# A hybrid stream encoder on one core: the order of the first loads, and the tiles that hold layer 0's last sums

## The chip, the cores and the metric

One Trainium2 chip, one of its cores. The metric is the device time of one execution of the whole program, in microseconds (us), as the median of several runs. A profiled execution gives the span (first to last instruction) and every instruction in it. The engines are called as in the profile: PE is TensorE (PEld its weight loads), DVE is VectorE, ACT is ScalarE, POOL is GpSimd, SP is SyncE, which issues most of the loads and stores of this kernel. A name with a q behind it (SPq, POOLq) is the sequencer of an engine, where DMA issues and waits are recorded.

## What is computed

One step of an encoder with two layers over 1024 prompt frames and 8 x 16 sample frames of width 1024. Layer 0 has its own keys and values and attends over a short window; layer 1 reads keys and values projected once, and attends over eight chunks of 64 before its own. Each layer ends in an MLP with squared ReLU. Cut to what matters here:

```python
def rmsnorm(x, g):
    xf = x.astype(jnp.float32)
    y = xf * lax.rsqrt(jnp.mean(xf * xf, axis=-1, keepdims=True) + EPS)
    return (y * g.astype(jnp.float32)).astype(x.dtype)

def mlp(x, g_norm, w_up, w_down):
    return jnp.square(jax.nn.relu(rmsnorm(x, g_norm) @ w_up)) @ w_down

for layer in range(DEPTH):
    if layer < N_LAYERS_A:
        qp, kp, vp = project_a(hp, g_attn[layer], w_qkv_a[i], g_q_a[i], g_k_a[i])
        ...
    else:
        kb_p, vb_p = shared_kv(hp, g_kv, w_kv, g_k_b)
        ...
    hp = hp + ap @ w_o
    hp = hp + mlp(hp, g_mlp[layer], w_up[layer], w_down[layer])
```

Everything is float32. `hp` is the residual of the prompt; the sample frames take the same steps.

## The kernel before

**Tiles.** The 1024 prompt frames are tiles 0 to 7 of 128 rows, the 128 sample frames are the ninth, `ST`. A matrix that feeds PE is split into a rounded high half and the rest as low half, and a product is made of three matmuls (high by high, high by low, low by high); `split` (L128 and L134) makes the halves, one on ACT or POOL, the other on DVE.

**The norm vectors.** The norm weights g are not applied to x but to the rows of the weight matrices. For this `prep_gains` (L1234) loads the five vectors (`g_attn` and `g_mlp` of both layers, `g_kv`) with five loads (L1243) into a tile of 40 x 128, turns it with a PE transposition (L1245) and copies it into `gcol` (L1246), one column for each 128 rows of each vector. The tile and its PSUM bank come from pools of their own, which are closed when the function ends; what is allocated next may come to lie in their place. The transposition needs the identity matrix: `run` loads it into `eye` (L1278), and DVE casts it to `identr` (L1280). All transpositions of x use it too.

**A weight.** `load_block` (L141) loads a weight in blocks of 256 rows (two k of 128) by 512 columns into a `raw` tile (L146). The raw tiles come from two pools in turn, `rawp` and, in layer 0, `ring` (tag `raw2`), two buffers each. `split_g` (L180) then multiplies each k with its column of `gcol`: the high half on POOL (L185), the low half on DVE (L190).

**The start of attention.** In layer 0, `attention` first calls, in this order of the code: `X(0)` (L1421, the load of x tile 0), the first block of the key and value weight, `X(1)`, `N(0)`, the second block, `X(ST)`, `N(1)`, the blocks three and four, `N(ST)`. `N` turns a tile of x (L210, eight transpositions), splits it into `hh` and `hl`, takes its sum of squares on ACT (Square, L201) and makes the scales of the tokens (L202, L1250 and L1254, the last on POOL). Then the constants follow (`sinks`, L1344 to L1353). The key and value projections `K1` of tiles 0, 1 and `ST` are interleaved: for each k the three matmuls of tile 0, then those of tile 1, and so on (L217 to L219). The query projections `Q1` of the same three tiles follow, with a weight of their own, then more tiles, scores and the rest of attention.

**Who orders the work.** The instructions of each engine are put in order at compile time, by a scheduler that runs a simulated timeline (`schedule_with_timeline_sim=True`); the engine then works its queue off in that order. `behind(a, b)` (L747) puts b after a in that order without making it wait for anything on the chip. A tile that takes the place of another one waits until the last reader of that one has finished (`reuse_waits="tile"`).

**The end of the MLP.** `mlp_down` multiplies with `w_down` in 40 products over two halves of the inner dimension, where sums of tokens and weights are formed so that fewer multiplications are needed. Each product has three banks (token tiles of a part; the parts are `PARTS = ((5, 6, 7), (2, 3, 4), (ST, 0, 1))`) and adds its result, with a sign, to some of six outputs o: output o belongs to part o // 2 and to the column half o % 2. The outputs are summed in SBUF tiles `x0` to `x8` where these are opened, and else the result is copied by ACT (L1162) and added to the residual in DRAM by a POOL DMA that accumulates (L1165 and L1179). The last two results are those of product 37 (output 0) and, in layer 0, of product 39, the last one (output 1). Both go, in the three token tiles of part 0, into the x tiles of part 2, which are done by then:

```python
if n > max(last[1:]) + 1:
    adds[o] = [xs[t][:, N[o % 2]] for t in PARTS[2]]
```

so into `x8` (`ST`), `x0` and `x1`. In layer 1 output 1 is opened at product 33 and does not come this way. `DOWN_HOME` (a list of tags) fixes which tile lies behind which in SBUF: ... `x8`, `x0`, `x2`, a gap of 640, `a0`, `x1`, `x3`, `x4` ... When layer 0 is over, the pools of layer 1's attention take the same place, in the order raw, weights, small tiles, `hpool` (`hh`, `hl`), work, ring, `apool` (`pth`, `ptl`, ...). By the sizes, `hh` and `hl` come to lie where `x8` and `x0` were, and `pth` and `ptl`, in which tile 1 is held, where the end of `x1`, `x3` and `x4` were.

## Time and profile before

| | us |
|---|---|
| median of 3 runs | 2357.6 |
| lowest and highest of them | 2350.82, 2359.93 |
| the profiled execution: its own time | 2354.01 |
| the profiled execution: span | 2352.2 |

The granted TensorE clock, as the mean of the profiled execution, was 0.997. Over the whole span the page shows these groups as the longest, with busy time, mean duration and idle time of the engine just before them:

```profile
L744 PE MATMUL ps_c<-w,a 128*128 128x512 f32 x960 | 374.7, 390 | 6.9 <-DVE w L134 6.9
L908 POOL DMA_DIRECT2D hd<-h x272 | 148.9, 550 | 594.8 <-ACT h L817 378.2
L128 ACT CAST a<-a 128x1536 fp32r<-128x1536 f32 x80 | 118.6, 1482 | 149.5 <-DMA a<-hd 149.5
L134 DVE TENSOR_TENSOR a<-a 128x1536 fp32r<-128x1536 f32 x80 | 140.5, 1756 | 45.7 <-ACT a L128 45.7
```

How such a line is read: the line of the kernel, the engine and operation, the tile written and the tiles read, the shape, how often; then busy us and mean ns of one; then how long the engine stood idle just before these instructions, and what it was released by. A row of a timeline has the start in us, the duration, the engine and the line; several alike instructions that follow each other are one row with their count. A row of the chain of waits has start, duration and what the time was spent in; "DMA a<-b" is a transfer from its issue until it let the next instruction go. Matmul durations overlap, so the pace of PE is the distance of two starts.

### The profile page before, as it was taken

Reading aid. Unit: us, or ns where it says so; the run is one execution under the profiler, and the core shown is the slowest. Engines: PE = TensorE matmul, PEld = TensorE weight load, DVE = VectorE, ACT = ScalarE, POOL = GpSimd, SP = SyncE. Lnnn points to the kernel's source line nnn. Section 1 sums busy time; section 2 is a strip of 40 time slices with the busy share of each in tenths; the row PEclk is TensorE's granted clock in tenths of the full one; section 3 lists DMA queues with packets and bytes.
Section 4 is the critical chain, followed back from the end, with each engine's and each line's share of the span. In section 5 each row is a group of like instructions: output and inputs, shape, how many; then the busy total and the mean of one; then the engine's idle time right before and its main releaser. Section 6 shows DMA issues by size and latency. Waiting matters only on the chain.

```text
span 2352.2 us, 33396 instructions
## 1 busy us (share of the span) xinstructions
PE 2271.4 (97%) x11429; PEld 1893.3 (80%) x11429; DVE 1715.4 (73%) x3075; ACT 1332.4 (57%) x2684; POOL 635.3 (27%) x950
## 2 busy tenths in 40 slices
PE   7998999899999999999999999998899999999999
PEld 6787887788888888777877788887788888888787
DVE  6788786766656578899577877777666566678987
ACT  3777674655555555344377666665655555565443
POOL 4334332313213111002333434344132132110011
PEclk9999999999999999999999999999999999999999
DMA  7335546234434677748653655555244343977567
GB/s 253 127 113 163 171 147 202 95 122 160 137 111 151 218 230 177 267 147 214 183 157 113 193 157 177 174 168 184 69 156 138 113 162 107 284 209 199 175 169 192
DMA packets 226715, 392.70 MB, mean 167 GB/s; under 512 B 51592, under 2 KB 126288, under 8 KB 226448
## 3 DMA queue, kind: packets, MB, share of 16 engines
q1 hardware_dynamic: 188816, 283.58, 37.4%
q0 software_dynamic: 36432, 102.26, 15.9%
q10 hardware_dynamic: 1296, 4.72, 0.5%
q8 instruction: 90, 1.47, 0.2%
q14 instruction: 81, 0.66, 0.1%
HBM read 236.51 MB, written 156.85 MB: 167 GB/s over the span
## 4 chain that ended last, share of the span: by engine, by line
PE 74%; DVE 9%; DMA 9%; ACT 3%; issue 3%; POOL 1%; SPq 0%; ACTq 0%; DVEq 0%; POOLq 0%
PE ps_c L743 6%; PE ps_c L744 6%; PE ps_c L745 6%; PE ps_x L743 5%; PE ps_x L745 5%; PE ps_x L744 5%; PE ps_mm L217 3%; PE ps_mm L219 3%; PE ps_mm L218 3%; PE ps_y L745 2%; PE ps_y L743 2%; PE ps_y L744 2%; PE ps_tr L324 2%; DMA a<-hd 2%; DVE w L134 1%
## 5 line engine op out<-in xcount | busy, mean ns | idle before, releaser
L744 PE MATMUL ps_c<-w,a 128*128 128x512 f32 x960 | 374.7, 390 | 6.9 <-DVE w L134 6.9
L743 PE MATMUL ps_c<-w,a 128*128 128x512 f32 x960 | 375.1, 391 | 5.1 <-DVE x L1174 3.1
L745 PE MATMUL ps_c<-w,a 128*128 128x512 f32 x960 | 374.3, 390 | 0.0
L908 POOL DMA_DIRECT2D hd<-h x272 | 148.9, 550 | 594.8 <-ACT h L817 378.2
L743 PEld LDWEIGHTS ps_c<-w,a 128*128 128x128 f32 x960 | 180.6, 188 | 46.3 <-issue 4.7
L744 PEld LDWEIGHTS ps_c<-w,a 128*128 128x128 f32 x960 | 180.7, 188 | 46.1 <-DVE w L134 9.0
L745 PEld LDWEIGHTS ps_c<-w,a 128*128 128x128 f32 x960 | 180.5, 188 | 37.5
L128 ACT CAST a<-a 128x1536 fp32r<-128x1536 f32 x80 | 118.6, 1482 | 149.5 <-DMA a<-hd 149.5
L217 PE MATMUL ps_mm<-w,hh 128*128 128x512 f32 x432 | 172.7, 401 | 8.8 <-POOL w L185 3.3
L134 DVE TENSOR_TENSOR a<-a 128x1536 fp32r<-128x1536 f32 x80 | 140.5, 1756 | 45.7 <-ACT a L128 45.7
L219 PE MATMUL ps_mm<-w,hl 128*128 128x512 f32 x432 | 171.7, 398 | 1.5 <-DMA hl<-hTd 1.4
L218 PE MATMUL ps_mm<-w,hh 128*128 128x512 f32 x432 | 170.8, 396 | 1.3 <-DVE w L190 1.1
L743 PE MATMUL ps_x<-sx,w 128*128 128x512 f32 (+1 forms) x408 | 157.8, 387 | 3.7 <-ACT h L864 2.7
L128 ACT CAST w<-s 128x2048 fp32r<-128x2048 f32 x56 | 107.1, 1912 | 92.2 <-DVE s L1060 80.7
L128 ACT CAST w<-ru 128x512 fp32r<-128x512 f32 (+1 forms) x160 | 110.0, 708 | 83.9 <-PE ps_y L744 32.0
L745 PE MATMUL ps_x<-sx,w 128*128 128x512 f32 (+1 forms) x408 | 154.1, 378 | 0.0
L744 PE MATMUL ps_x<-sx,w 128*128 128x512 f32 (+1 forms) x408 | 154.1, 378 | 0.0
L134 DVE TENSOR_TENSOR w<-s,w 128x2048 fp32r<-128x2048 f32 x56 | 128.1, 2288 | 32.4 <-ACT w L128 32.3
L1179 POOL DMA_DIRECT2D xp<-o x28 | 36.3, 1296 | 411.8 <-ACT o L1162 390.2
L134 DVE TENSOR_TENSOR ptl<-ps_tr,pth 128x512 fp32r<-128x512 f32 x180 | 122.4, 685 | 24.1 <-ACT pth L128 18.2
L134 DVE TENSOR_TENSOR w<-ru,w 128x512 fp32r<-128x512 f32 (+1 forms) x160 | 126.6, 793 | 14.7 <-ACT w L128 14.6
L816 ACT ACTIVATE h<-h 128x512 f32<-128x512 f32 (+1 forms) x102 | 61.9, 607 | 122.6 <-DVE h L866 93.5
(274 smaller groups left out, 6131.4 us busy)
## 6 DMA issues: line engine op xcount, KB each, us to landing
a<-hd SPq DMA_DIRECT2D x80, 768.0 KB, 6.2
hd<-h POOLq DMA_DIRECT2D x272, 192.0 KB, 2.5
ru<-in_w_up SPq DMA_DIRECT2D x64, 512.0 KB, 3.9
r<-in_w_down SPq DMA_DIRECT2D x32, 1024.0 KB, 10.0
xp<-o POOLq DMA_DIRECT2D x28, 768.0 KB, 9.4
o<-oTd SPq DMA_DIRECT2D x50, 256.0 KB, 5.0
x<-xp SPq DMA_DIRECT2D x23, 512.0 KB, 5.2
xp<-xo SPq DMA_DIRECT2D x18, 512.0 KB, 2.8
```

The costliest lines, as they stand in the source:

```text
L128: a = nc.scalar.copy(hi, src)
L134: return a, e.tensor_tensor(lo, src, hi.bitcast(F32), ALU.subtract)
L217: nc.tensor.matmul(ps, a, w[:, 0, k, :], start=(k == 0), stop=False)
L218: nc.tensor.matmul(ps, a, w[:, 1, k, :], start=False, stop=False)
L219: self.lp = nc.tensor.matmul(ps, b, w[:, 0, k, :], start=False, stop=(k == KC - 1))
L324: self.lp = nc.tensor.transpose(pt[:, i, :], get(i), self.ident)
L743: a = mm(ps, ah, bh, start=first, stop=False, skip_group_check=True)
L744: mm(ps, ah, bl, start=False, stop=False, skip_group_check=True)
L745: return a, mm(ps, al, bh, start=False, stop=last, skip_group_check=True)
L816: a = nc.scalar.activation(t, src, AF.Relu)
L908: return lambda p, z: self.nc.gpsimd.dma_start(self.hd[c // 4][:, p, c % 4], z)
L1179: nc.gpsimd.dma_start(dst, z, accum_op=ALU.add)
```

## The change

Two places. In the opening, the identity is no longer loaded in `run`. `prep_gains` is called from `attention` right behind `X(0)`, loads the identity, then the five vectors with three loads (both layers of `g_attn` in one, both of `g_mlp` in one, `g_kv`), all put behind x tile 0 in SP's order. Its tile is now a slot of the scratch tag of `work`, its bank the `m` bank of attention. The first weight block is put behind the last of these loads, and x tile 1 behind the first weight block. In `mlp_down`, the results of the very last product go into the x tiles 1, 3 and 4 instead of `ST`, 0 and 1; what they are added to in DRAM stays the same.

```diff
@@ load_block
-            nc.sync.dma_start(raw, wr[:, k0 : k0 + 2, n0 : n0 + 512])
+            self.ld = nc.sync.dma_start(raw, wr[:, k0 : k0 + 2, n0 : n0 + 512])
@@ mlp_down
-                            adds[o] = [xs[t][:, N[o % 2]] for t in PARTS[2]]
+                            home = (1, 3, 4) if n == total - 1 else PARTS[2]
+                            adds[o] = [xs[t][:, N[o % 2]] for t in home]
@@ prep_gains
-    def prep_gains(self):
+    def prep_gains(self, first):
         nc, I = self.nc, self.ins
-        with ExitStack() as st:
-            self.psum_pools(st, "pg", dict(m=(1, 1)), dict(m="m"))
-            tmp = self.pool(st, "tmpg")
-            g = tmp.tile([5 * KC, P], F32, tag="g", name="g")
-            for i, v in enumerate(
-                (I["g_attn"][0], I["g_attn"][1], I["g_mlp"][0], I["g_mlp"][1], I["g_kv"])
-            ):
-                nc.sync.dma_start(g[i * KC : (i + 1) * KC, :], v.rearrange("(k p) -> k p", p=P))
-            ps = self.psum("m", [P, 5 * KC], "ps_g")
-            nc.tensor.transpose(ps, g, self.ident[0 : 5 * KC, 0 : 5 * KC])
-            nc.vector.tensor_copy(self.gcol, ps)
+        z = [nc.sync.dma_start(self.eye, I["eye"])]
+        nc.vector.tensor_copy(self.identr, self.eye)
+        g = self.scratch([P, 4, P], F32, "g")[0 : 5 * KC, 0]
+        rows = lambda a: a.rearrange("l (k p) -> (l k) p", p=P)
+        z.append(nc.sync.dma_start(g[0 : 2 * KC], rows(I["g_attn"])))
+        z.append(nc.sync.dma_start(g[2 * KC : 4 * KC], rows(I["g_mlp"])))
+        z.append(nc.sync.dma_start(g[4 * KC : 5 * KC], I["g_kv"].rearrange("(k p) -> k p", p=P)))
+        for a in z:
+            self.behind(first, a)
+        ps = self.psum("m", [P, 5 * KC], "ps_g")
+        nc.tensor.transpose(ps, g, self.ident[0 : 5 * KC, 0 : 5 * KC])
+        nc.vector.tensor_copy(self.gcol, ps)
+        return z[-1]
@@ run
-            eye = cp.tile([P, P], F32, tag="eye", name="eye")
-            nc.sync.dma_start(eye, I["eye"])
+            self.eye = cp.tile([P, P], F32, tag="eye", name="eye")
             self.identr = cp.tile([P, P], F32R, tag="identr", name="identr")
-            nc.vector.tensor_copy(self.identr, eye)
...
-            self.prep_gains()
@@ attention
-                nc.sync.dma_start(xr[t], x_src(t))
+                return nc.sync.dma_start(xr[t], x_src(t))
...
-                X(0)
+                z = self.prep_gains(X(0))
                 self.load_block(wkv, wkv_src, kv0, gkv, [0])
-                X(1)
+                self.behind(z, self.ld)
+                self.behind(self.ld, X(1))
                 N(0)
```

## The prediction

> **What bounds the kernel now.** I read the page's busy shares first, then the windows over the opening and over the border between the two layers, then the timeline of each engine and the chain of waits there.

> ```profile
> span 2352.2 us, 33396 instructions
> PE 2271.4 (97%) x11429; PEld 1893.3 (80%) x11429; DVE 1715.4 (73%) x3075; ACT 1332.4 (57%) x2684; POOL 635.3 (27%) x950
> ...
> 0.00:4.20 4.20, 0.00 (x0) 0.01 (x1) 0.29 (x2) 1.28 (x1) 0.41 (x5) 1.00 0.16 32
> 4.20:6.50 2.30, 0.30 (x1) 0.17 (x1) 0.20 (x1) 0.04 (x1) 0.00 (x0) 1.00 0.91 333
> 10.40:13.50 3.10, 0.00 (x0) 0.00 (x0) 2.42 (x4) 0.44 (x1) 3.02 (x5) 1.00 0.94 352
> 13.50:15.80 2.30, 1.22 (x2) 0.50 (x2) 2.30 (x4) 0.00 (x0) 2.30 (x3) 1.00 0.48 170
> 15.80:20.00 4.20, 4.17 (x11) 3.33 (x12) 4.20 (x8) 1.15 (x2) 2.72 (x3) 1.00 0.41 140
> 20.00:35.00 15.00, 15.00 (x72) 12.48 (x71) 8.86 (x19) 3.12 (x7) 5.37 (x9) 1.00 1.05 394
> 35.00:54.60 19.60, 17.85 (x88) 14.69 (x86) 12.79 (x28) 7.46 (x19) 11.05 (x11) 1.00 0.56 173
> ```

> The columns of a window are its length, then busy time of PE, PEld, DVE, ACT and POOL, granted clock, DMA share, GB/s. TensorE is busy 97% of the span, so time is to be had only where it idles: 2352.2 - 2271.4 = 80.8 us in all. The first 4.2 us move 32 GB/s, and from 10.4 to 13.5 TensorE does nothing at all while the DMA engines are 94% busy. From 20 to 35 it has no gap. A start that comes earlier is therefore worth what it brings forward, if the stage after it stays fed.

> ```profile
> 0.74 0.39 SPq L1278 DMA_DIRECT2D eye<-in_eye  x1
> 2.94 0.83 SPq L1421 DMA_DIRECT2D x<-in_x_prompt  x2
> 3.81 0.43 SPq L146 DMA_DIRECT2D raw<-in_w_qkv_a  x1
> ...
> 2.60 1.49 DMA g<-in_g_kv
> ...
> 4.22 0.31 PE ps_g L1245
> ...
> 4.55 7.19 DMA raw<-in_w_qkv_a
> ...
> 2.64 0.23 DVE L1280 CAST identr<-eye 128x128 fp32r<-128x128 f32 x1 [1.76 <-DMA eye<-in_eye]
> 6.57 3.65 PE L210 MATMUL ps_n<-identr,x 128*128 128x128 f32 x16 [2.06 <-DMA x<-in_x_prompt]
> 7.70 0.59 ACT L128 CAST hh<-ps_n 128x512 fp32r<-128x512 f32 x1
> 10.48 1.36 POOL L185 TENSOR_SCALAR w<-raw,gcol 128x512 fp32r<-128x512 f32 x2 [2.02 <-DMA raw<-in_w_qkv_a]
> 11.81 0.98 POOL L1254 TENSOR_TENSOR rx<-vx,mhalf 128x1 f32<-128x1 f32 x1
> 12.78 0.69 POOL L185 TENSOR_SCALAR w<-raw,gcol 128x512 fp32r<-128x512 f32 x1
> 13.50 5.56 DVE L190 SCALAR_TENSOR_TENSOR w<-raw,gcol,w 128x512 fp32r<-128x512 f32 x5
> 13.52 1.22 PE L217 MATMUL ps_mm<-w,hh 128*128 128x512 f32 x2 [3.30 <-POOL w L185]
> 15.83 0.79 PE L218 MATMUL ps_mm<-w,hh 128*128 128x512 f32 x1 [1.08 <-DVE w L190]
> ```

> Two things are seen. The identity and five norm rows are issued before x, so x is issued at 2.94. And the second weight load is issued at 4.55, just as the transposition of the norm rows ends: the chain runs from g over ps_g to that load. I read this as the norm tile of `prep_gains` lying where the first `raw` buffer comes to lie. So the load that could go at 3.81 is the block in the other buffer (`raw2`, rows k = 2, 3), and the first block, k = 0, 1, is the one of 4.55, which lands at 4.55 + 7.19 = 11.74. The matmuls agree: the first one starts not after the two weight products of 10.48 but after the third (12.78 + 0.69 = 13.47), and its low half waits for the third L190 (five of them take 5.56, so 13.50 + 2 x 1.1 = 15.7).

> **The change, part one: the opening.** Moved to the front: x tile 0, from 2.94 to 0.74. Behind it in SP's queue come the identity, three norm loads instead of five, the first weight, x tile 1. Six issues filled 0.74 to 2.94, 0.37 us each: identity 1.1, norms 1.5 to 2.2, first weight about 2.6, x tile 1 about 3.0. Nothing is queued behind a wait, since none of these waits for an engine.

> x tile 0 was used at most 6.57 - 2.94 = 3.6 us after its issue, so it lands at about 4.3. The identity took 2.64 - 0.74 = 1.9 us alone; now its bytes follow x's, so 4.5, cast 0.23, and the transpositions start at 4.75 instead of 6.57: 1.8 us earlier. The high half of tile 0, at 7.70 to 8.29 before, is then done by 6.5.

> The norm rows land by about 4.6 (1.49 us after the last issue, and behind x), plus 0.31 for ps_g and 0.2 for its copy: 5.1 instead of 4.75. That is later, and costs nothing as long as the first weight lands after it, a cover of about 1 us; without the cover it costs up to that 0.4. Two fewer loads on SP save 0.7 us of issue, which is in the times above. The scratch slot and the one bank of PSUM that the norm rows now borrow are free again by 5.1, before the first projection wants them.

> Four loads of 512 KB landed between 6.5 (x 0) and 11.74 (first weight), so (11.74 - 6.5) / 3 = 1.75 us each. Now: x 0 at 4.3, the first weight at 6.2, x 1 at 8.0, the other weights at 9.7, 11.5, 13.2. The first weight product ends at 6.2 + 0.69 = 6.9, its low half on DVE at 8.0. The projections of tiles 0 and 1 are interleaved row by row, so PE then stands at tile 1: x 1 at 8.0, the 1.2 us that passed between tile 0's landing (6.5) and its first cast (7.70), and the cast of 0.59 give 9.8, and the low half on DVE about 10.4. What is late next is therefore x tile 1, no longer the weight. The steady stream that began at 15.83 begins at about 10.4: 5.4 us earlier. DVE does not hold it: its product takes 1.1 us for a row that gives PE six matmuls.

> ```profile
> 24.86 9.33 DMA raw<-in_w_qkv_a
> ...
> 34.27 1.36 POOL w L185 x2
> ...
> 29.58 0.47 ACT L276 ACTIVATE VS<-ps_mm,rx 128x256 fp32r<-128x256 f32 x1 [0.66 <-PE ps_mm L219]
> 16.42 0.63 PE L219 MATMUL ps_mm<-w,hl 128*128 128x512 f32 x1
> 16.84 0.63 PE L218 MATMUL ps_mm<-w,hh 128*128 128x512 f32 x1
> 19.54 0.39 PE L219 MATMUL ps_mm<-w,hl 128*128 128x512 f32 x1
> 19.77 0.40 PE L217 MATMUL ps_mm<-w,hh 128*128 128x512 f32 x1
> ```

> Does the next stage stay fed? Tiles 0 and 1 are projected by 29.58; the sample tile's 24 matmuls at 19.77 - 19.54 = 0.23 us follow, to about 35; then the queries, whose last weight pair is wanted 18 matmuls later, about 39. It lands at 34.2, and a product of 0.69 and a low half of 1.1 later, about 36, it can be used. The slack is 3 us. So if the query weights come no earlier than now, 3.0 us of the 5.4 survive; the DMA engines are full there (394 GB/s from 20 to 35), but only 140 to 170 GB/s were moved between 13.5 and 20, and the raw buffers come free earlier with the products. I take 5.0, with 3.0 as the low bound and, from the first weight product (13.47 to 6.9), 6.6 as the high one.

> **Part two: the last sums of layer 0.** They occur once, at the last of 40 products; in layer 1 the half concerned is already opened there, so nothing changes.

> ```profile
> 1135.52 0.86 POOL L1165 DMA_DIRECT2D xp<-x  x1 [7.10 <-ACT x L1162]
> 1138.30 0.85 POOL L1165 DMA_DIRECT2D xp<-x  x1 [1.92 <-ACT x L1162]
> 1139.87 1.94 PE L210 MATMUL ps_n<-identr,x 128*128 128x128 f32 x16
> 1141.11 0.85 POOL L1165 DMA_DIRECT2D xp<-x  x1 [1.96 <-ACT x L1162]
> 1142.63 1.07 ACT L128 CAST hh<-ps_n 128x512 fp32r<-128x512 f32 x2 [1.96 <-DMA xp<-x]
> 1143.36 0.47 PE L217 MATMUL ps_mm<-w,hh 128*128 128x512 f32 x1 [1.55 <-ACT hh L128]
> 1147.84 1.08 ACT L128 CAST hh<-ps_n 128x512 fp32r<-128x512 f32 x2 [4.14 <-DMA xp<-x]
> ```

> Three adds into DRAM read the tiles of the sample and of 0 and 1; layer 1's first `hh`/`hl` take the place of the first two, so ACT waits 1.96 us for an add to land and PE 1.55 us for ACT. With the sums in tiles 1, 3 and 4 those two places are last read two products earlier (the sums of the other half), and ACT can cast at 1142.63 - 1.96 = 1140.67. Gain at most 1.55. What is late next: the second tile's casts wait for the third add, landed at 1147.84, and by the sizes in the code tiles 3 and 4 lie where these buffers come to lie, so that wait stays. PE, starting its 24 matmuls (5.5 us) at 1141.8, would be done at 1147.4 and then stand about 0.6 to 1.1 us. Number of copies and adds unchanged: 0. Bounds 0 and -1.55; I take -1.0.

> **Sum.** -5.0 - 1.0 = -6.0 us against the profiled execution's 2354.0 (span 2352.2), so 2348.0; the median of the runs shown, 2357.6, stands 3.6 above it, so 2351.6, given as 2351.5. From the bounds alone: 2357.6 - 8.15 = 2349.5 to 2357.6 - 3.0 = 2354.6.

> **Rivals.**

> Late query weights: the part-one gain stops at the slack of 3.0 and the border gives nothing: 2354.6. For it: DMA share 1.05 from 20 to 35. Against: the low traffic before 20.

> [...]

> ```profile
> 400.00:450.00 50.00, 43.71 (x260) 36.33 (x259) 43.02 (x63) 28.57 (x52) 21.11 (x18) 1.00 0.31 109
> ...
> 1600.00:1700.00 100.00, 88.04 (x537) 75.35 (x536) 68.00 (x102) 56.63 (x117) 32.40 (x31) 0.97 0.34 114
> ```

> Another order further on. The order of the queues is chosen by a simulated timeline, which starts differently now, and attention's order may come out otherwise. These two rows are the largest stalls, 6.3 and 12.0 us of PE idle. A new stall like the larger, added to -6.0, gives +6.0: 2363.6; it decides from 6 us up. The same effect with luck, one stall of 6.3 closed besides: -12.3, 2345.3. Nothing in the profile speaks for either; most later stages are chained to PE and would only move.

> The change does not do what it says: the norm tile still holds back a weight, x 0 alone gains 1.8, its use waits for the weight: 2357.

> **How the numbers follow.** Forecast 0.50; late query weights 0.14; colder start 0.04; another order, slower 0.11, faster 0.16; not done 0.05. The likeliest gives 2351.5, its own range 2349.5 to 2354.6 before the spread of medians (the runs shown span 9 us, so about 4 each way). With the other cases the range is 2340 to 2362. 0.5% is 11.8 us, about what a measurement of this kernel can tell from no change. Faster than 2345.8: most of the lucky order and the tail of the forecast, 0.23. Slower than 2369.4: a stall beyond 18 us, 0.06. Within: 0.71.

> **What would show it.** x 0 issued at about 0.74 and transposed at about 4.8; the first weight product at 6 to 7, the first matmul near 7, the stream from about 10.4, and the projections of tiles 0 and 1 done near 24 instead of 29.6. At the border ACT's first cast not released by the add, the idle of 1.55 gone and a smaller one before the second tile. The forecast is wrong if the stream begins after 13, if PE idles between 24 and 40, or if the border's and the opening's gains are seen but the stages between them have other lengths.

## The result and the profile after

The change made the kernel slower. Ten runs of the changed kernel have a median of 2368.07 us (2360.59 to 2377.28), ten of the kernel before 2357.74 (2350.82 to 2362.4): ratio 1.0047, 95% interval 1.003 to 1.0064. Nine more runs of it, beside 33 of the kernel before, gave 1.0035 (1.002 to 1.005). The mean of the two ratios is 1.0041, some 9.7 us of loss where 6 of gain were forecast.

The busy shares of the page of the changed kernel; its profiled execution took 2371.51 us, at a mean granted clock of 0.988:

```profile
span 2369.7 us, 33389 instructions
PE 2287.0 (97%) x11429; PEld 1907.0 (80%) x11429; DVE 1716.9 (72%) x3075; ACT 1330.7 (56%) x2684; POOL 633.6 (27%) x950
```

TensorE's idle time is 2369.7 - 2287.0 = 82.7 us, only 1.9 more than before, while the span is 17.5 longer. The rest is busy time: the same 11429 matmuls kept TensorE busy for 15.6 us more. Hold on to that; it is the half of the answer that an idle count doesn't show.

The opening, in the timeline of the changed kernel (start, duration, engine, line, work, and in brackets the idle time before it with its releaser):

```profile
0.74 0.38 SPq L1421 DMA_DIRECT2D x<-in_x_prompt  x1
2.58 0.37 SPq L1243 DMA_DIRECT2D g<-in_g_kv  x1
2.99 0.41 SPq L146 DMA_DIRECT2D raw<-in_w_qkv_a  x1
...
5.97 0.30 PE L1247 MATMUL ps_g<-identr,g 40*128 40x40 f32 x1 [5.97 <-DMA g<-in_g_kv]
6.20 1.97 PE L210 MATMUL ps_n<-identr,x 128*128 128x128 f32 x8
8.04 0.78 PE L217 MATMUL ps_mm<-w,hh 128*128 128x512 f32 x1
10.17 0.77 PE L218 MATMUL ps_mm<-w,hh 128*128 128x512 f32 x1
...
25.13 0.50 PE L219 MATMUL ps_mm<-w,hl 128*128 128x512 f32 x1 [2.27 <-DVE hl L134]
...
50.58 0.66 PE L260 MATMUL ps_q<-identr,qr 128*128 128x128 f32 x4 [1.80 <-DVE qr L239]
```

The stream of matmuls starts at 10.17 instead of 15.83, and the first transpositions of queries, at 54.65 in the timeline of before, stand at 50.58: 4.1 us earlier. The opening does what it was meant to do.

Where the lead goes is read by following some instructions, found by their line and their number on it, through both timelines:

| start of | before | after | difference | after, second execution | difference |
|---|---|---|---|---|---|
| first transposition of queries (L260) | 54.65 | 50.58 | -4.1 | 50.67 | -4.0 |
| first probability product (L331) | 71.13 | 68.63 | -2.5 | 67.10 | -4.0 |
| last probability product of layer 0 (L332) | 374.55 | 384.01 | +9.5 | 380.15 | +5.6 |
| first product of the MLP (L743, `ps_x`) | 430.78 | 435.42 | +4.6 | 431.56 | +0.8 |
| last sum product of layer 0 (L745, `ps_c`) | 1139.64 | 1149.51 | +9.9 | 1145.87 | +6.2 |
| first probability product of layer 1 | 1198.48 | 1216.18 | +17.7 | 1209.61 | +11.1 |
| end of the span | 2352.2 | 2369.7 | +17.5 | 2363.2 | +11.0 |

The second execution is the profile of whole_change_again, the same kernel. Two stretches lose that the change has reordered: the attention of layer 0 (up to the first product of the MLP) and the border of the layers. The attention's loss must not be read at its last probability product: the new order only puts that product later, 51.4 us ahead of the MLP where before has 56.2. The MLP between the two stretches is longer too, by 5.2 and 5.5 us, though its order is the same; over the 14 profiles of this study it takes 708.9 us (before, the shortest of all) to 716.1, so how much of that is chance stays open. Behind the border nothing more is lost.

Windows (length, then busy time of PE, PEld, DVE, ACT, POOL, granted clock, DMA share, GB/s), first two of before, which go with the rows of before in the prediction:

```profile
300.00:400.00 100.00, 95.79 (x509) 78.12 (x508) 73.14 (x206) 61.94 (x167) 31.16 (x53) 1.00 0.57 187
1140.00:1199.00 59.00, 55.18 (x286) 46.11 (x285) 37.66 (x103) 27.32 (x75) 22.83 (x33) 1.00 0.65 207
```

Then the changed kernel:

```profile
300.00:400.00 100.00, 90.91 (x463) 73.17 (x462) 65.34 (x183) 54.96 (x152) 28.28 (x50) 0.97 0.52 167
400.00:450.00 50.00, 46.23 (x260) 37.59 (x258) 44.48 (x65) 28.63 (x52) 21.27 (x20) 1.00 0.35 127
1600.00:1700.00 100.00, 87.96 (x527) 74.94 (x526) 71.96 (x124) 58.15 (x129) 37.45 (x37) 0.95 0.38 127
1140.00:1217.00 77.00, 70.19 (x331) 59.10 (x330) 40.15 (x105) 29.27 (x77) 25.80 (x35) 0.91 0.53 159
```

At 300 to 400 and at the border TensorE both idles more and runs at a lower clock: 0.97 and 0.91 as the mean of these windows, against 1.00 in before. In the 14 profiles of this study, from 30 us on, the lower clock comes as stretches of one or two times 3.41 us at 0.50 to 0.52, and outside of them it is 0.98 to 1.00 (the last section); half pace means these stretches. The two places in the timeline, first the attention, one row of before and three of the changed kernel:

```profile
364.47 0.47 PE L176 MATMUL ps_mm<-w,oh 128*128 128x512 f32 x1 [1.55 <-DVE xo L1614]
```

```profile
351.12 0.50 PE L176 MATMUL ps_mm<-w,oh 128*128 128x512 f32 x1 [2.04 <-DVE xo L1614]
367.55 0.47 PE L176 MATMUL ps_mm<-w,oh 128*128 128x512 f32 x1 [1.76 <-DVE xo L1614]
372.51 0.33 PE L605 MATMUL ps_utp<-identr,sp 128*128 128x128 f32 x1 [1.89 <-ACT sp L601]
```

Three waits of about 2 us, where before had one over 1 us in this stretch, that of 1.55; the second execution has two, of 1.48 and 2.05. What in the new order makes them isn't shown. Then the border, one row of before and the changed kernel:

```profile
1153.82 0.18 DVE L627 TENSOR_SCALAR gq<-gq 128x64 f32<-128x64 f32 x1
```

```profile
1150.99 0.85 POOL L1166 DMA_DIRECT2D xp<-x  x1 [1.96 <-ACT x L1163]
1149.72 0.44 SPq L625 DMA_DIRECT2D gq<-in_g_q_b  x1
1151.47 2.04 ACT L128 CAST hh<-ps_n 128x512 fp32r<-128x512 f32 x4
1152.19 0.47 PE L217 MATMUL ps_mm<-w,hh 128*128 128x512 f32 x1 [0.51 <-ACT hh L128]
1155.58 0.20 DVE L627 TENSOR_SCALAR gq<-gq 128x64 f32<-128x64 f32 x1 [14.34 <-DMA gq<-in_g_q_b]
1156.21 1.28 DVE L134 TENSOR_TENSOR hl<-ps_n,hh 128x512 fp32r<-128x512 f32 x2
1156.95 1.11 PE L210 MATMUL ps_n<-identr,x 128*128 128x128 f32 x4 [4.05 <-DVE hl L134]
```

ACT's casts no longer wait for an add, and TensorE's wait for them has gone from 1.55 to 0.51. But DVE now has layer 1's multiply of the query norm weights (`gq`, L627) ahead of the first low halves. It waits for a load issued at 1149.72, the low halves wait behind it in DVE's queue, and TensorE stands for 4.05 us after two matmuls. In before that multiply came 9 instructions later, at 1153.82, and waited for nothing. The chain of waits of the changed kernel shows why the load is there so soon:

```profile
1145.40 3.78 DMA xp<-x
...
1149.72 5.74 DMA gq<-in_g_q_b
...
1155.58 0.10 DVE gq L627
```

The first of the three adds lets the small tiles' place go, and the load leaves at once; in before it left at 1148.10, 8.5 us after the last sum product, here 0.2 us after it.

Put in order of time, the matmuls of a trace show how far the order of the work moved: of the 11429, compared by tile and shape, before and after differ at places 10 to 75 (the opening), 1003 to 2155 (attention of layer 0, about 200 to 380 us) and 5490 to 5604 (the border). With part one alone the first two regions differ, with part two alone only the third; the two executions of the changed kernel have one and the same order.

### The profile page after: what moved, and what is told of

It reads as the page before. It is cut to its first block, busy times and chain, and to the rows that moved or that the text cites. A ratio compares the mean times of both kernels' runs of the same rounds, so it can differ in the third digit from the quotient of the medians.

```text
span 2369.7 us, 33389 instructions
## 1 busy us (share of the span) xinstructions
PE 2287.0 (97%) x11429; PEld 1907.0 (80%) x11429; DVE 1716.9 (72%) x3075; ACT 1330.7 (56%) x2684; POOL 633.6 (27%) x950
## 4 chain that ended last, share of the span: by engine, by line
PE 77%; DVE 9%; DMA 8%; ACT 3%; issue 2%; POOL 1%; SPq 0%; ACTq 0%; DVEq 0%; POOLq 0%
PE ps_c L743 7%; PE ps_c L744 7%; PE ps_c L745 7%; PE ps_x L743 5%; PE ps_x L745 5%; PE ps_x L744 5%; PE ps_mm L217 4%; PE ps_mm L219 4%; PE ps_mm L218 3%; PE ps_y L745 2%; PE ps_y L743 2%; PE ps_y L744 2%; DMA a<-hd 2%; PE ps_tr L324 2%; PE ps_mm L176 1%
## 5 line engine op out<-in xcount | busy, mean ns | idle before, releaser
L743 PE MATMUL ps_c<-w,a 128*128 128x512 f32 x960 | 375.5, 391 | 4.6 <-DVE x L1175 2.7
L745 PE MATMUL ps_c<-w,a 128*128 128x512 f32 x960 | 374.9, 391 | 0.0
L743 PEld LDWEIGHTS ps_c<-w,a 128*128 128x128 f32 x960 | 180.9, 188 | 45.2 <-issue 3.8
L745 PEld LDWEIGHTS ps_c<-w,a 128*128 128x128 f32 x960 | 181.0, 189 | 37.4
L128 ACT CAST a<-a 128x1536 fp32r<-128x1536 f32 x80 | 118.6, 1482 | 142.8 <-DMA a<-hd 142.7
L217 PE MATMUL ps_mm<-w,hh 128*128 128x512 f32 x432 | 174.1, 405 | 5.6 <-ACT kw L284 1.8
L219 PE MATMUL ps_mm<-w,hl 128*128 128x512 f32 x432 | 173.5, 402 | 3.8 <-DVE hl L134 2.3
L218 PE MATMUL ps_mm<-w,hh 128*128 128x512 f32 x432 | 171.9, 399 | 0.2
L743 PE MATMUL ps_x<-sx,w 128*128 128x512 f32 (+1 forms) x408 | 158.7, 389 | 3.9 <-ACT h L864 2.7
L128 ACT CAST w<-s 128x2048 fp32r<-128x2048 f32 x56 | 107.1, 1912 | 93.9 <-DVE s L1060 85.8
L128 ACT CAST w<-ru 128x512 fp32r<-128x512 f32 (+1 forms) x160 | 110.0, 708 | 82.1 <-PE ps_y L744 32.0
L745 PE MATMUL ps_x<-sx,w 128*128 128x512 f32 (+1 forms) x408 | 155.1, 380 | 0.0
```

Of the source, the lines that this page charges most:

```text
L128: a = nc.scalar.copy(hi, src)
L217: nc.tensor.matmul(ps, a, w[:, 0, k, :], start=(k == 0), stop=False)
L218: nc.tensor.matmul(ps, a, w[:, 1, k, :], start=False, stop=False)
L219: self.lp = nc.tensor.matmul(ps, b, w[:, 0, k, :], start=False, stop=(k == KC - 1))
L743: a = mm(ps, ah, bh, start=first, stop=False, skip_group_check=True)
L745: return a, mm(ps, al, bh, start=False, stop=last, skip_group_check=True)
```

## The experiments

Theory A: the two parts work as forecast, and the loss is the price of the two reorderings that the scheduler's timeline made out of them. Rival B: the moved loads and sums themselves cost it, by transfers that collide later. It also had to be found whether the lower clock is a cause or a consequence. All twelve kernels were timed in three groups of four, each beside the same runs of the kernel before: 29 (median 2360.6), 35 (2361.2) and 33 (2360.1).

| kernel | median us | ratio to before | 95% |
|---|---|---|---|
| opening_only | 2363.36 | 1.0015 | 1.0001 to 1.003 |
| sums_only | 2365.72 | 1.0020 | 1.0007 to 1.0032 |
| order_of_before | 2359.94 | 0.9996 | 0.9981 to 1.0011 |
| order_of_after | 2375.20 | 1.0055 | 1.0036 to 1.0074 |
| gq_behind | 2366.60 | 1.0019 | 1.0006 to 1.0033 |
| attention_order_of_before | 2365.73 | 1.0020 | 1.0007 to 1.0032 |
| opening_order_of_before | 2359.14 | 0.9995 | 0.9982 to 1.0009 |
| opening_busy_in_waits | 2357.49 | 0.9986 | 0.9974 to 0.9998 |
| whole_change_again | 2367.60 | 1.0035 | 1.002 to 1.005 |
| both_reorderings_mended | 2359.35 | 0.9993 | 0.998 to 1.0006 |
| before_busy_in_six_waits | 2354.68 | 0.9976 | 0.9966 to 0.9986 |
| opening_busy_in_six_waits | 2356.02 | 0.9974 | 0.9961 to 0.9988 |

**Each part alone.** opening_only is the changed kernel with the last sums back in `PARTS[2]`; sums_only is the kernel before with this one edit:

```diff
-                            adds[o] = [xs[t][:, N[o % 2]] for t in PARTS[2]]
+                            home = (1, 3, 4) if n == total - 1 else PARTS[2]
+                            adds[o] = [xs[t][:, N[o % 2]] for t in home]
```

> The opening is changed, the last sums stay in the tiles of ST, 0 and 1. Theory O (order): the change pays in the opening (-4.1 us up to the first scores) and loses because the scheduler puts layer 0's attention in another order (the last value product of layer 0 comes 9.5 us late instead of 4.1 early); the border between the layers, which costs 7.8 us in the changed kernel, goes back to before (58.9 us from the last product of layer 0 to the first value product of layer 1). So about 2368.1 - 7.8 = 2360. Theory C (clock alone): the order is neutral and TensorE's half-pace windows of 3.4 us fall where they fall; then this kernel has about the time of the changed one, 2368, or of the one before, 2358, and the stretch of attention shows no other idle time.

> The opening stays as before, the last sums of layer 0 go into the tiles 1, 3 and 4. Theory O: only the order at the border differs from before, and it costs what it costs in the changed kernel: DVE's multiply of g_q stands ahead of tile 0's low halves and waits for its load; PE idles 4 us there instead of 1.55 and then runs at half pace; 58.9 us become about 66.7, the time about 2365.5. Theory R (the release of the tiles gains as predicted, and the border of the changed kernel was a chance of its run): 2356 to 2358.

Both parts lose alone: 0.0015 and 0.0020 of 2360.6 are 3.5 and 4.7 us, together 8.2, about the whole. So there is not one culprit. In the trace of opening_only the first probability product comes 4.6 us earlier than in before and the first product of the MLP 1.8 later; in that of sums_only the border holds a wait of 4.31 us.

**The order held.** order_of_before is the changed kernel with every instruction behind the first key and value projections chained, on each of the five engines, in the order of the kernel before; order_of_after is the code of before with the changed kernel's order. The links put instructions in sequence at compile time and make nothing wait on the chip (the profile of order_of_before counts 33389 instructions, as that of the changed kernel):

```diff
+    def pin(self):
...
+        made = self.nc.cur_bb.bb.instructions[self.seen :]
...
+            line = [made[i] for i in np.cumsum(steps.astype(np.int32))]
+            for a, b in zip(line, line[1:]):
+                self.tc.add_manual_dep(b, a.name, AFTER, reason="order")
```

> Both parts of the change, but every instruction after the first key and value projections stands on its engine in the order that it had before; no wait is added or taken away by that. Theory O: the losses in attention and at the border vanish and the gains stay, -4 in the opening and -1 to -1.5 at the border: about 2353, and about 2.5 us of PE idle less before 55 us. Theory D (the earlier start itself does harm, by transfers that now collide, or by stretches that PE begins cold): about 2368 as with the change, or above 2361 at least.

> Neither part of the change; but every instruction after the first key and value projections stands in the order that the changed kernel has. Theory O: the losses come without the gains: about 2368 + 4 = 2372, with the wait of 4 us for DVE at the border (there the last sums release the first tiles late as before, so it may be longer). Theories C and D: the order does nothing by itself, about 2358.

As to the loss this settles A against B. The changed loads and sums in the old order cost nothing (0.9996); the old loads and sums in the new order cost 13 us (1.0055), more than the change itself, and the border in that trace holds waits of 1.55 and 7.23 us, as its expectation had allowed. But the two parts don't work as forecast: in the old order the change gains almost nothing. Two places of order_of_before show what the lead meets. First near 345 us, the timeline of before, then that of order_of_before:

```profile
343.21 0.32 SPq L1616 DMA_DIRECT2D xp<-xo  x1
346.09 0.33 SPq L1603 DMA_DIRECT2D xo<-in_x_prompt  x1
349.71 0.69 DVE L1614 TENSOR_TENSOR xo<-ps_mm,xo 128x512 f32<-128x512 f32 x1 [0.86 <-DMA xo<-in_x_prompt]
```

```profile
340.61 0.32 SPq L1625 DMA_DIRECT2D xp<-xo  x1
345.80 0.33 SPq L1612 DMA_DIRECT2D xo<-in_x_prompt  x1
349.35 0.69 DVE L1623 TENSOR_TENSOR xo<-ps_mm,xo 128x512 f32<-128x512 f32 x1 [3.10 <-DMA xo<-in_x_prompt]
```

The store of `xo` leaves 2.60 us earlier, but the load that needs its buffer leaves only 0.29 earlier: the store took 5.2 us to let it go, against 2.9 before. A lead of 2.6 us meets a transfer that isn't as early, and TensorE waits 2.13 us for `xo` where before it had waited under 0.5. Then the border of order_of_before:

```profile
1141.97 0.85 POOL L1175 DMA_DIRECT2D xp<-x  x1 [1.97 <-ACT x L1172]
1150.27 1.29 DVE L134 TENSOR_TENSOR hl<-ps_n,hh 128x512 fp32r<-128x512 f32 x2 [6.95 <-issue]
1151.02 0.50 PE L219 MATMUL ps_mm<-w,hl 128*128 128x512 f32 x1 [2.40 <-DVE hl L134]
```

The first tile starts without any wait; the low halves of tile 1 come 8.3 us after the third add is issued, and TensorE stands 2.40. The row names no releaser ("issue"); that it is the third add is read from the places of the tiles (`ptl` behind the end of `x4`) and from the next group. From the last sum product to the first probability product of layer 1 the border takes 60.8 us here, against 58.3 to 58.9 in the five profiles that have both the old tiles and the old order: by the traces part two loses some 2 us even with the order held.

**The two reorderings one at a time.** gq_behind moves only the multiply at the border; attention_order_of_before holds the order only up to the end of layer 0 (the same list, cut where layer 1 begins):

```diff
-            self.split(hh[half], hl[half], ps)
+            self.lo = self.split(hh[half], hl[half], ps)[1]
...
-            self.nc.vector.tensor_scalar(t, t, mul, None, ALU.mult)
+            z = self.nc.vector.tensor_scalar(t, t, mul, None, ALU.mult)
+            if self.hold is not None:
+                self.behind(self.hold, z)
...
                 N(1, "pt")
+                self.hold = self.lo
```

> The changed kernel whole, with one thing moved in layer 1: VectorE's multiply of the query norm weights by -0.125, which in the changed kernel stands ahead of the first tile's low halves and there waits for its transfer (TensorE idle 4.05 us behind the first two matmuls of the layer), goes behind the low halves of tile 1. Theory A, that this multiply makes the stall at the border: the stall behind the first two matmuls falls under 1 us, the stretch from the last sum product of layer 0 to the first probability product of layer 1 (66.3 us) falls to some 61 to 63, the time to 2363 to 2365. Theory B, that the accumulating transfer of the last sums makes it in any order: the stall stays at 3 to 4 us, now at tile 1, and the time at 2366 to 2369.

> The changed kernel whole, with the order of every engine's instructions in the first layer behind the first products held as in the kernel before; the border and layer 1 keep the changed kernel's order. If the two reorderings (attention of layer 0, border) cost their price separately: 2359.9 for the order of before everywhere plus some 5 for the border, 2364 to 2366, and the attention of layer 0 ends at 375 us, not 384. If the attention's order is worth nothing in the end because later stretches make it up: 2367 to 2369. If the border alone costs nothing: 2359 to 2361.

Against the whole change (1.0041, the mean of its two ratios) gq_behind is lower by 0.0022 and attention_order_of_before by 0.0021: some 5 us each, each known to about 4 us. In microseconds gq_behind's 2366.6 lies where B of its expectation had it; I had set that range by a median of another group, and the ratio is the fairer measure. Its timeline at the border decides:

```profile
1144.81 0.85 POOL L1169 DMA_DIRECT2D xp<-x  x1 [1.97 <-ACT x L1166]
1145.91 1.29 DVE L135 TENSOR_TENSOR hl<-ps_n,hh 128x512 fp32r<-128x512 f32 x2
1155.01 1.07 ACT L129 CAST hh<-ps_n 128x512 fp32r<-128x512 f32 x2 [7.60 <-DMA xp<-x]
1155.09 1.29 DVE L135 TENSOR_TENSOR hl<-ps_n,hh 128x512 fp32r<-128x512 f32 x2 [2.89 <-issue]
1155.83 0.80 PE L220 MATMUL ps_mm<-w,hl 128*128 128x512 f32 x1 [2.58 <-DVE hl L135]
```

The wait of 4.05 is gone, as A had it: the first tile's low halves start at 1145.91, at once. Behind it a wait of 2.58 comes to light at tile 1, 10.3 us after the third add was issued; ACT's next casts start at the same moment, and their row names the add. B named that wait too. So both were there, one behind the other. For the attention the traces say the same as the ratio, a little lower: from the first transposition of queries to the MLP, the nine profiles with the old order take 375.1 to 380.7 us, the five with the new one 379.5 to 384.8.

> The whole change with both mends at once: the attention of layer 0 in the order of the kernel before, and layer 1's multiply of the query norm weights behind the low halves. If the two reorderings are all of the loss and their prices add up: no more than 2 us from the kernel before, 2359 to 2363; the border then still holds one stall of some 2.5 us, at tile 1's low halves, that wait for the third accumulating transfer. If there is a third cause: over 2364.

> The changed kernel as it is, run beside the next three, so that all four stand against the same runs of the kernel before. If the loss is the change's own: 8 to 15 us over the kernel before (the ratio 1.0047 with its interval 1.003 to 1.0064, times some 2361 us: 2368 to 2376). If it was the chip or the hour: within 5 us of the kernel before.

both_reorderings_mended is gq_behind with the held order of attention: 0.9993, level with before, while the whole change beside it lost 0.0035, some 8 us. The order of the attention and the place of that one multiply are the whole loss. The wait at tile 1 is there as expected, with 1.59 us.

**The opening with the order held, and the clock.** opening_order_of_before is part one with the old order behind it. The next kernel adds 28 matmuls to it, ahead of two of TensorE's waits; their results are overwritten:

```diff
+        if self.npv == 25:
+            self.busy(pv[:, 0:256], self.KT[:, self.at[0], self.at[1], :, :], FILL)
         self.nc.tensor.matmul(pv, v, pts[0], start=first, stop=False)
...
+    def busy(self, out, mv, n):
+        nc = self.nc
+        z = [nc.tensor.matmul(out, self.identr, mv, start=True, stop=True).ins for _ in range(n)]
```

> Part one alone (the opening), with every later instruction in the order of the kernel before, the last sums of layer 0 where the kernel before has them. If the 4.3 us of the opening last to the end where no order changes: 2355 to 2357. If they are given back at later waits whatever the order (the wait for the tile xo near 350 us, whose load did not leave earlier in the run with the order of before): 2359 to 2361.

> The kernel of opening_order_of_before with 28 more matmuls (128x256, results overwritten): 14 ahead of the probability product that waits 2.07 us for pth near 203 us, 14 ahead of the first scores of layer 1 that wait 2.24 us for qT near 1182 us; they leave of these waits under 0.6 us idle and end before the wait would. If half pace follows from TensorE's idle time in one interval of 3.41 us (over 1.85 us idle): no half pace within 10 us behind either wait, where it followed the first in 6 of 6 profiles and the second in 3 of 6, and the time is 1.5 to 3 us under that of opening_order_of_before. If half pace has another cause (transfers, the other engines' load, chance): it still follows the first wait, and the time is the same within 1 us, or 1 to 3 us higher where the added matmuls delay the waiting ones.

The first is the second case of its expectation: 2359.1, level within the noise with before (0.9982 to 1.0009), not 2355 to 2357. The lead is mostly given back. For the second, the windows and the wait near 200 us, first of opening_order_of_before:

```profile
199.45:202.86 3.41, 1.60 (x10) 1.24 (x11) 3.41 (x9) 3.41 (x12) 2.54 (x4) 1.00 0.16 42
202.86:206.27 3.41, 3.41 (x9) 2.55 (x9) 3.21 (x8) 3.39 (x10) 2.21 (x3) 0.50 0.61 173
```

then of opening_busy_in_waits, windows and timeline:

```profile
199.58:203.00 3.42, 2.31 (x15) 1.55 (x13) 3.42 (x10) 3.42 (x14) 2.25 (x3) 1.00 0.13 33
203.00:206.41 3.41, 3.41 (x16) 2.60 (x15) 3.21 (x9) 3.38 (x7) 2.59 (x3) 1.00 0.61 170
```

```profile
198.14 1.84 PE L760 MATMUL ps_pv<-KT,identr 128*128 128x256 f32 x14
200.87 0.51 PE L336 MATMUL ps_pv<-pth,VS 128*128 128x512 f32 x1 [0.89 <-ACT pth L130]
```

Without the added matmuls TensorE idles 3.41 - 1.60 = 1.81 us of one window and does the next at half pace, 9 matmuls where the other kernel does 16. With them 0.89 of the wait is left (I had expected under 0.6), and the next window is at full pace. At the other wait 0.59 is left and the pace stays full as well, but there it had stayed full in the profile of opening_order_of_before too. Over all profiles it is clearer: half pace follows the wait near 200 us in 10 of the 11 without added matmuls, and in none of the three with them.

Over the runs the mean granted clock rose from 0.9933 to 0.9954, and the median time fell by 1.65 us. Each run lists its span and mean granted clock; span times (1 - clock) is the time lost to the clock. That fell by 4.9 us (15.7 to 10.8), but the rest of the spans rose by 3.3 (2341.4 to 2344.7), for a reason that isn't shown; and the intervals of the two ratios overlap. So the clock's part is shown here, the gain in time is not.

The last two kernels carry 70 such matmuls, 42 of them ahead of four waits of the sum products of layer 0, into a PSUM bank that the code sets aside there and does not use; one on the kernel before, in its own order, one on opening_order_of_before:

```diff
+BUSY_AT = {7774: 10, 7931: 10, 8485: 14, 8528: 8}
...
+        self.busy_here("z")
         mm(ps, ah, bl, start=False, stop=False, skip_group_check=True)
```

> The kernel before, in its own order throughout, with 70 matmuls added whose results are not used: 14 ahead of the probability product near 205 us, 14 ahead of the first scores of layer 1 near 1181 us, and 10, 10, 14 and 8 (128x128) ahead of the four sum products of layer 0 that wait 1.4, 1.2, 1.6 and 2.2 us in the profile of before (974.72, 1001.42, 1103.00, 1113.86). If half pace follows from TensorE's idle time in one interval of 3.41 us: the mean granted clock rises from 0.9935 to 0.996 or more, and the time falls by 3 to 6 us, to 2355 to 2358. If it does not: no change in the clock, and the time within 2 us of the kernel before or above it.

> Part one alone with every later instruction in the order of the kernel before, and the same 70 added matmuls. By the idle time in an interval: 1.5 to 3.5 us under opening_busy_in_waits (2357.5), 2353 to 2356, and 1 to 4 us under before_busy_in_six_waits, which lacks the opening. If the opening's gain is given back at later waits whatever the clock does: level with before_busy_in_six_waits within 1 us.

The kernel before with 70 matmuls more is 5.6 us faster by the ratio: 0.9976 (0.9966 to 0.9986). One of the waits, first in before, then in this kernel:

```profile
1103.00 0.47 PE L743 MATMUL ps_c<-w,a 128*128 128x512 f32 x1 [1.60 <-DVE x L1174]
```

```profile
1106.88 1.67 PE L767 MATMUL ps_busy<-identr 128*128 128x128 f32 x14
1108.87 0.47 PE L752 MATMUL ps_c<-w,a 128*128 128x512 f32 x1 [0.31 <-DVE x L1214]
```

TensorE works in most of the wait, and 0.31 us of it are left. Not every one was filled: at the first of the four sum products 1.60 and 1.59 us are left idle in the profiles of the two kernels, and half pace follows it in both. The time lost to the clock has a mean of 16.5 us for the kernel before and 11.6 for this one, and what is left of the spans is the same, 2342.4 and 2342.0. So here the gain is the clock alone (0.9930 to 0.9951, less than the 0.996 I had asked for). opening_busy_in_six_waits, with 0.9974, is level with it, as the second case of its expectation has it. Both beat the kernel before and the changed one.

## Why the prediction was wrong

**The opening** was right in its mechanism, and its sizes were close. x tile 0 was issued at 0.74 as said, and x and the cast identity were there at 4.35 and 4.78, as forecast. The transpositions began at 6.20, not 4.75: they stand behind the transposition of the norm rows, whose last load took 3.4 us from its issue and not 1.49. The first matmul came at 8.04, not near 7, the stream at 10.17 against 10.4, and 4.1 us were left at the queries against 5.0 taken. The slack to the query weights held; what opened was a gap of 2.27 at 25.13 for the sample tile's low halves, in the stretch that the prediction had named as the place of a failure; by 50 us 1.6 of the 5.7 us that the stream had gained are gone, net.

**That this lead reaches the end** was assumed and is what failed next. With the order held, the opening is worth 0.0005 of the time by one pair (opening_order_of_before) and 0.0002 by the other (0.9974 against 0.9976): about 1 us and not 4 to 5. The intervals of the two pairs taken together leave room for some 3 us of gain; order_of_before and both_reorderings_mended, 0.0004 and 0.0007 under before, carry part two as well. The trace of order_of_before shows one taker, the store and load of `xo`. That it is the main one isn't shown: in the traces of the six kernels with the opening and the old attention order, the attention of layer 0 ends 2.8 to 5.6 us earlier than in before in four and level in two. One execution moves that end by some 2 us: sums_only and before_busy_in_six_waits, with the old opening and the old order, have it at 377.24 and 376.80, not 374.55. Against the latter, opening_busy_in_six_waits is 5.0 us ahead there, 3.7 ahead at the first probability product of layer 1 and 3.4 behind at the end; in between TensorE waits 2.98 us for a load of `hl`. Where the lead goes in most runs stays open.

**Part two** was right about the wait it removes: 1.55 us fell to 0.51 in the changed kernel and to nothing in order_of_before. The term for what is late next, "about 0.6 to 1.1 us" before the second tile, was too small: 2.40, 2.58 and 1.59 in the three traces where nothing hides it. It took the third add's landing from before (6.7 us after its issue), and the reader was let go only 8.3, 10.3 and 9.3 us after it; the stores and weights of layer 1 start earlier beside it, but that they are the reason isn't shown. So the net of -1.0 has the wrong sign: in these three traces the border is some 2 to 5 us longer than with the old tiles and the old order.

**The step that failed** is the rival "another order further on", and its last sentence: "Nothing in the profile speaks for either; most later stages are chained to PE and would only move." In the sum this stands as a term of nothing for all that comes behind the opening and the border's first waits. The order did come out otherwise, in stretches of some 1150 and 115 of TensorE's places, and it cost about 5 us in the attention and 5 at the border. The rival had 0.11 for one new stall of 12 us; what came was several of 2 to 4 us. Something did speak for it: the prediction shows rows where the next instruction of an engine waits for a transfer, and a new order can put a cheap instruction with a fresh load (`gq`, whose buffer the first add frees earlier now) ahead of the halves. The prediction followed the tiles that were moved, but not what else lies in the places they set free.

**A stall's price** was taken as its own length. In this kernel a wait of 2 us in TensorE can cost some 3.7: its own length and the 1.71 us that the next 3.41 us lose where they run at half pace, as they did after all 71 intervals with 1.9 us of idle time or more (the last section). In the group of the repeated run, 19.5 us are lost to the clock in the changed kernel and 16.5 in the kernel before, so 3 of its loss of 8 to 9.

**The other rivals.** Late query weights: no. A colder start, a longer slow stretch of the opening than in before: no, before's matmuls start 0.43 us apart from 16.42 to 18.55, those of the changed kernel 0.23 from 11.15 on; half pace did come, but at 52 us, with starts 0.43 apart until 55.15. The 0.04 it was given was the author's estimate, which the trace of the changed kernel doesn't bear out; what the profiles show ahead of half pace is in the table at the end. Not done: no, the chain from g to the first weight is gone.

## What to carry to other kernels

Where a scheduler derives the order from a simulated timeline, an edit at the start edits the whole program: compare the order of each engine's instructions first, and hold the old order to see what the edit itself is worth. When a buffer is set free earlier, look at everything that lies in it: a cheap operation with a late load that moves ahead in a queue can cost more than the wait that was removed (here TensorE stood 4.05 us behind `gq`, and the other wait fell by 1.04, from 1.55 to 0.51). And where TensorE must wait about 2 us, work whose result is thrown away can be cheaper than idling: here six such places, waits of 1.18 to 2.24 us in before, were worth 5.6 us.

## What the hardware showed that was not expected

| idle time in the interval, us | intervals | next at half pace |
|---|---|---|
| under 1.2 | 9075 | 1 |
| 1.2 to 1.4 | 79 | 2 |
| 1.4 to 1.8 | 99 | 18 |
| 1.8 to 1.9 | 18 | 13 |
| 1.9 and more | 71 | 71 |

An interval of 3.413 us at a clock of 0.50 loses 1.71 us. So in these profiles a wait of 2 us is charged or not by where the grid happens to cut it, and the grid lies at another place in almost every one. The runs without a profile show no grid, only their mean clock: over the 29 runs of the kernel before in the first group the mean clock varied from 0.990 to 0.997, and time and clock go together with a correlation of -0.76 (-0.76 and -0.52 in the other two groups). The two timelines that the whole study started from were one of a lucky execution (before, clock 0.997, 7 us lost) and one of an unlucky one (after, 0.988, 28 us), which is why they stand 17.5 us apart and the medians 10.
